# Where the embedding product of a transformer layer is computed: in the gate stage, or for nine of ten token tiles between the rounds of the attention

## The chip, the cores and the metric

The kernel runs on one core of one Trainium2 chip. Its time is the device time of one execution in microseconds (us). Three runs of the kernel before took 1705.35 to 1705.85 us, with a median of 1705.7 us. The engines are named as in the profile: PE is TensorE (matmuls; PEld are its weight loads), DVE is VectorE, ACT is ScalarE, POOL is GpSimd, and SP is SyncE, whose queue issues nearly all DMAs.

## The reference

One layer of a bidirectional encoder is applied to 1024 and 256 tokens of width 1024, all in float32. What matters here, cut short:

```python
h = h + concat(diff_attention, gqa_attention) @ w_out   # both from one input projection
h = h + square(relu(norm(h) @ w_ff1)) @ w_ff2
gate = sigmoid(norm(h) @ w_ple_gate)
h = h + gate * (p @ w_ple_proj)        # p: tokens x 256, w_ple_proj: 256 x 1024
y = norm(h)
```

The last product, `p @ w_ple_proj`, is the embedding product. It depends on two inputs alone, so it can be computed at any time.

## The kernel before, in words

There are ten token tiles of 128 tokens (TORD, line 851, is their order). Each float32 matrix product is made of three matmuls on operands that are split into a high and a low part: high by high, high by low, low by high. ScalarE makes the high part by a rounding copy, and VectorE or GpSimd the low part by a subtraction.

The stages follow each other: the input projections, the attention, the MLP's two products (done by a scheme with seven products in place of eight, and kept in DRAM in between), and the gate stage.

**The attention** (lines 515 to 1060) runs in rounds. `plan_unit` (line 600) puts the steps of each unit of 256 queries into numbered rounds: scores `sc` on TensorE (line 642), their maximum or distance penalty on VectorE (lines 655 and 659), exponentials on ScalarE (lines 664 and 667), the scaling by the sum on GpSimd (675, 681), transposes `tr` on TensorE (696), their split by ScalarE (702) and VectorE (707), and the product with the values, `av` (720). Loads of keys and queries are issued three rounds ahead of the scores that use them (line 633).

**The side work.** A round leaves TensorE time, since the other engines work on the scores. A generator, `side_work` (line 954), gives other matmuls for it: first the rest of the query and key projections, `qk_rest` (line 814, tile `psa`), then the output projection in two parts (line 887, tile `pso`), of which the second needs the finished attention. The main loop (line 1037) first emits the round's scores, transposes and softmax steps, then takes side work until the debt is paid, and then emits the `av` products and the ends. The debt is the round's cost on TensorE, plus a constant for each `av` step, times `RATIO` (0.43) for rounds under 160, and times `RATIO2` (0.6) after that. A `yield 0.0` of the generator ends the side work of the round. Whatever is left of the second part of the output projection runs after the attention (line 1213), together with the transposes of the MLP's input.

In what order each engine takes its instructions is decided when the program is built: a scheduler places each instruction by a simulated time and the program's order, and each engine then takes its own list in that order and waits at the head of it.

**The gate stage** (lines 1546 to 1633) takes one token tile after another. `gate_input` (line 1499) transposes the next tile's residual and splits it. `gate` (1568) makes 24 matmuls of 512 columns for each half of the tile (tile `psg`) and then a sigmoid on ScalarE, VectorE and GpSimd. `embed` (1588) makes the half's embedding product in PSUM, of six matmuls (tile `psp`). Its operands are the token tile of p, loaded and split in the loop (lines 1552 to 1557), and the two row blocks of the weight, which `proj_w` (1486) has split while the MLP ended. `add` (1598) multiplies the product by the gate (VectorE, line 1601), updates the residual and takes its squares. Then the tile is normalised and stored. The last tile is cut into three pieces, and its embedding products are placed behind its gate products.

## Time and profile before

| what | value |
|---|---|
| median of three runs | 1705.7 us |
| span of the profiled execution | 1703.2 us |
| TensorE busy | 1666.5 us (98%), 9849 matmuls |
| VectorE, ScalarE, GpSimd busy | 1177.2, 868.3, 658.4 us |
| score matmuls | from 196.3 us to 686.1 us |
| matmuls of the output projection | from 446.6 us to 753.9 us |
| gate matmuls | from 1547.1 us to 1690.5 us |
| moved by DMA | 278.28 MB |

The profile is that of one execution; its times count from the start of the span. The profiled execution has no time of its own beside the span; what lies around the span is read from the difference between the span and the runs' median, 2.5 us. A row of the groups gives busy time and the mean duration of one instruction, and behind a bar the idle time of the engine before it. The end of a matmul is modelled, and successive matmuls overlap, so that the time that one costs is read from how many fit into a stretch.

### The profile page before, as it was taken

Reading aid. Unit: us, or ns where it says so; the run is one execution under the profiler, and the core shown is the slowest. Engines: PE = TensorE matmul, PEld = TensorE weight load, DVE = VectorE, ACT = ScalarE, POOL = GpSimd, SP = SyncE. Lnnn points to the kernel's source line nnn. Section 1 sums busy time; section 2 is a strip of 40 time slices with the busy share of each in tenths; the row PEclk is TensorE's granted clock in tenths of the full one; section 3 lists DMA queues with packets and bytes.
Section 4 is the critical chain, followed back from the end, with each engine's and each line's share of the span. In section 5 each row is a group of like instructions: output and inputs, shape, how many; then the busy total and the mean of one; then the engine's idle time right before and its main releaser. Section 6 shows DMA issues by size and latency. Waiting matters only on the chain.

```text
span 1703.2 us, 27269 instructions
## 1 busy us (share of the span) xinstructions
PE 1666.5 (98%) x9849; PEld 1488.6 (87%) x9849; DVE 1177.2 (69%) x2119; ACT 868.3 (51%) x1749; POOL 658.4 (39%) x647
## 2 busy tenths in 40 slices
PE   8999999999899999999999999999999999999997
PEld 8999889888788888889999999998888888888886
DVE  7788588787887878578666666665655865445666
ACT  8543377677766767674333233333433333354644
POOL 1224455555653445424655666520533400001441
PEclk9999999999999999999999999999999999999999
DMA  9767844433953624495343434359666466532111
GB/s 316 228 225 246 233 141 124 138 92 108 269 156 118 165 69 127 134 308 181 132 156 127 138 131 150 122 198 376 202 216 195 130 205 193 169 114 73 35 44 50
DMA packets 191867, 278.28 MB, mean 163 GB/s; under 512 B 13674, under 2 KB 121076, under 8 KB 191732
## 3 DMA queue, kind: packets, MB, share of 16 engines
q1 hardware_dynamic: 189988, 271.28, 49.7%
q0 software_dynamic: 1600, 5.24, 1.0%
q8 instruction: 78, 1.28, 0.3%
q14 instruction: 57, 0.47, 0.1%
q10 hardware_dynamic: 144, 0.00, 0.0%
HBM read 182.63 MB, written 88.61 MB: 159 GB/s over the span
## 4 chain that ended last, share of the span: by engine, by line
PE 79%; DVE 7%; ACT 4%; issue 4%; DMA 3%; POOL 3%; SPq 0%; POOLq 0%; ACTq 0%; DVEq 0%
PE psa L255 6%; PE sc L642 5%; PE psb L255 5%; PE av L720 5%; PE pso L255 4%; PE tr L696 3%; PE psv L255 3%; PE psg L1576 2%; DVE pl L707 1%; DMA h_sb<-in_x 1%; DVE mm L659 1%; PE f__16295 L156 1%; PE f__15255 L156 1%; PE f__16637 L156 1%; PE f__15600 L156 1%
## 5 line engine op out<-in xcount | busy, mean ns | idle before, releaser
L1373 ACT ACTIVATE ao<-ar 128x1280 fp32r<-128x1280 f32 x56 | 71.3, 1275 | 187.5 <-PE f__16299 L156 37.8
L642 PE MATMUL sc<-kt,qt 128*128 128x512 f32 (+1 forms) x576 | 157.0, 392 | 6.9 <-ACT p L667 4.6
L707 DVE TENSOR_TENSOR pl<-tr,ph 128x512 fp32r<-128x512 f32 x204 | 137.9, 684 | 33.5 <-ACT ph L702 32.3
L1375 DVE TENSOR_TENSOR ao<-ar,ao 128x1280 fp32r<-128x1280 f32 x56 | 93.3, 1666 | 94.0 <-ACT ao L1373 94.0
L702 ACT ACTIVATE ph<-tr 128x512 fp32r<-128x512 f32 x204 | 119.8, 595 | 56.9 <-PE tr L696 50.4
L255 PE MATMUL pso<-ow,mt 128*128 128x512 f32 x480 | 119.4, 395 | 4.2 <-ACT ow L883 1.8
L696 PE MATMUL tr<-ident,p 128*128 128x128 f32 x768 | 116.0, 274 | 5.7 <-DVE pl L707 4.9
L642 PEld LDWEIGHTS sc<-kt,qt 128*128 128x128 f32 x576 | 99.4, 190 | 24.8 <-ACT p L667 6.1
L1576 PE MATMUL psg<-gw,n 128*128 128x512 f32 (+1 forms) x504 | 115.4, 384 | 0.0
L696 PEld LDWEIGHTS tr<-ident,p 128*128 128x128 f32 x768 | 91.8, 141 | 22.5 <-DVE pl L707 8.6
L1576 PEld LDWEIGHTS psg<-gw,n 128*128 128x128 f32 x504 | 90.8, 188 | 19.5
L255 PEld LDWEIGHTS pso<-ow,mt 128*128 128x128 f32 x480 | 87.5, 188 | 22.4 <-DVE osq L747 2.0
L1094 POOL TENSOR_SCALAR w1r<-w1r,gmlp 128x256 f32<-128x256 f32 x112 | 79.7, 728 | 67.6 <-DMA w1r<-in_w_ff 67.6
L720 PE MATMUL av<-ph,vt 128*128 128x256 f32 x544 | 102.4, 289 | 1.1 <-ACT ph L702 0.5
L681 POOL TENSOR_SCALAR p<-p,rl 128x1024 f32<-128x1024 f32 x64 | 76.0, 1188 | 51.3 <-DVE rl L679 46.6
L1167 ACT ACTIVATE w<-w1s 128x512 fp32r<-128x512 f32 x56 | 35.2, 628 | 116.5 <-POOL w1s L1174 49.4
L659 DVE TENSOR_REDUCE mm<-sc 128x1 f32<-128x1024 f32 (+1 forms) x80 | 84.2, 1055 | 8.8 <-PE sc L642 8.3
L720 PE MATMUL av<-pl,vt 128*128 128x256 f32 x408 | 89.5, 301 | 0.0
L720 PEld LDWEIGHTS av<-ph,vt 128*128 128x128 f32 x544 | 82.4, 190 | 6.6 <-ACT ph L702 0.9
L667 ACT ACTIVATE p<-sc,mm 128x1024 f32<-128x1024 f32 x64 | 71.3, 1114 | 25.5 <-DVE mm L659 18.5
L655 DVE CUSTOM_DVE_ANT_0 p<-sc,dist 128x1024 f32<-128x1024 f32 x64 | 77.6, 1218 | 7.9 <-PE sc L642 3.8
L664 ACT ACTIVATE p<-p,mm 128x1024 f32<-128x1024 f32 x64 | 73.5, 1149 | 18.0 <-DVE mm L655 17.3
(1520 smaller groups left out, 4717.2 us busy)
## 6 DMA issues: line engine op xcount, KB each, us to landing
ar<-ad SPq DMA_DIRECT2D x56, 640.0 KB, 4.0
w2r<-in_w_ff SPq DMA_DIRECT2D x56, 512.0 KB, 4.6
qt<-qd SPq DMA_DIRECT2D x160, 128.0 KB, 3.1
ad<-q SPq DMA_DIRECT2D x64, 320.0 KB, 3.0
ad<-qs SPq DMA_DIRECT2D x48, 320.0 KB, 2.2
w1r<-in_w_ff SPq DMA_DIRECT2D x28, 512.0 KB, 4.3
md<-ml SPq DMA_DIRECT2D x40, 256.0 KB, 2.5
mt<-md SPq DMA_DIRECT2D x20, 512.0 KB, 5.4
```

Of the source, the lines that this page charges most:

```text
L255: PE.matmul(ps, a, b, start=i == 0, stop=i == n - 1)
L642: PE.matmul(ps[:, h0:h0 + n], shared["q"][:, cc, v, i * P:(i + 1) * P], kt[:, s0 + h0:s0 + h0 + n], start=v == 0, stop=v == 1)
L655: V.tensor_tensor_reduce(out=p[:, :sn], in0=ps[:, :sn], in1=dst_t[:, off:off + sn], scale=SLOPES[idx], scalar=3.0e38, op0=ALU.add, op1=ALU ...
L659: V.tensor_reduce(out=st["m", i][:, 0:1], in_=ps[:, :sn], axis=AX.X, op=ALU.max, negate=True)
L681: G.tensor_scalar(p[:, :sn], p[:, :sn], rl[:, 0:1], 1.0, op0=ALU.mult, op1=ALU.mult)
L696: PE.transpose(t[:, jj, i * P:(i + 1) * P], st["ws"][i][:, j * P:(j + 1) * P], ident)
L702: S.activation(ph, st["tr", j2], AF.Copy)
L707: V.tensor_tensor(pl, st["tr", j2], f(st["ph", j2][:]), op=ALU.subtract)
L720: PE.matmul(st["av"][:, :256], x_, y_, start=j2 == 0 and n == 0, stop=j2 == nj - 1 and n == len(pr) - 1)
L1094: G.tensor_scalar(raw[:, k], raw[:, k], gmlp[:, 4 * kh + k:4 * kh + k + 1], 1.0, op0=ALU.mult, op1=ALU.mult)
L1375: V.tensor_tensor(ao[:, 1], a, f(ao[:, 0]), op=ALU.subtract)
L1576: ends[:] = [PE.matmul(ps, a, b, start=m == 0, stop=m == len(pr) - 1)]
```

## The change

A new generator, `embed_early`, stands in the side work between `qk_rest` and the output projection. It loads the projection weight by halves of 512 columns and pT by pairs of token tiles, splits them on ScalarE and GpSimd, makes the six matmuls of each tile and half (tile `pse`), evacuates the product from PSUM on ScalarE (tile `eo`), and stores it to `ed` in DRAM. It skips the token tile that the gate stage takes last. The gate stage loads each other tile's product into one of two slots (`et`) and multiplies by it from SBUF; it makes the embedding product itself for the last tile alone. The split of the weight for that tile moves from the end of the MLP into the gate stage. `RATIO` goes from 0.43 to 0.5. The early load of one part of the MLP's weight, which the main loop issued when the first output tile was done, is issued behind the attention if it has not been by then.

```diff
-    RATIO = 0.43
+    RATIO = 0.5
...
+    ed = dp.tile([NT, P, D], F32, name="ed")
+
+    def embed_early():
+
+        out = [wp.tile([P, 4, P], F32R, tag=tag, name="eo") for tag in ("wh", "wl")]
+        wt = [wp.tile([P, 4, P], F32R, tag=tag, name="ew") for tag in ("wh", "wl") * 2]
+
+        def half(n0):
+            for k in range(2):
+                raw = rawp.tile([P, 4, P], F32, tag="raw", name="rawe", bufs=2)
+                dma(raw, w_proj[k * P:(k + 1) * P, n0:n0 + 512].rearrange("p (a c) -> p a c", c=P))
+                yield 0.0
+                S.activation(wt[2 * k], raw, AF.Copy)
+                G.tensor_tensor(wt[2 * k + 1], raw, f(wt[2 * k][:]), op=ALU.subtract)
+
+        def tokens(t0):
+            raw = rawp.tile([P, 4, P], F32, tag="raw", name="rawe", bufs=2)[:].rearrange("p (k c) t -> p k (c t)", k=2)
+            dma(raw, pT[:, t0:t0 + 256].rearrange("(k p) t -> p k t", p=P))
+            hl = zp.tile([P, 2, 512], F32R, tag="zl", name="pe").rearrange("p v (k t) -> p v k t", k=2)
+            S.activation(hl[:, 0], raw, AF.Copy)
+            G.tensor_tensor(hl[:, 1], raw, f(hl[:, 0]), op=ALU.subtract)
+            return hl
+
+        w = [t[:].rearrange("p a c -> p (a c)") for t in wt]
+        pairs = [(n0, t0) for n0 in range(0, D, 512) for t0 in range(0, T, 256)]
+        hls = []
+        for i, (n0, t0) in enumerate(pairs):
+            if t0 == 0:
+                yield from half(n0)
+            while len(hls) < 2 and i + len(hls) < len(pairs):
+                hls.append(tokens(pairs[i + len(hls)][1]))
+            hl = hls.pop(0)
+            for u in range(2):
+                t = t0 // P + u
+                if t == LASTT:
+                    continue
+                c = slice(u * P, u * P + P)
+                ps = pj("pse")
+                pr = []
+                for k in range(2):
+                    pr += [(hl[:, 0, k, c], w[2 * k]), (hl[:, 0, k, c], w[2 * k + 1]), (hl[:, 1, k, c], w[2 * k])]
+                yield from mm_gen(ps, pr, 3)
+
+                def evac(ps=ps, t=t, n0=n0, o=out[u]):
+                    o = f(o[:].rearrange("p a c -> p (a c)"))
+                    S.activation(o, ps, AF.Copy)
+                    dma(ed[t, :, n0:n0 + 512], o)
+
+                if u == 0:
+                    evac()
+                else:
+                    deferred.append(evac)
+                    yield 0.0
...
     def side_work():
         yield from qk_rest()
+        yield from embed_early()
         flush()
...
     flush()
+    if not WN[0]:
+        w1_fetch(0, 1)
...
-            proj_w(0, AOS[m % 3])
-            proj_w(1, WOS[m % 3])
             n3[FORD[1]] = gate_input(FORD[1])
...
-        pr_ = gq_.tile([P, 2, P], F32, tag="pr", name="pr")
-        dma(pr_, pT[:, t * P:(t + 1) * P].rearrange("(k p) t -> p k t", p=P))
-        p_h = gq_.tile([P, 2, P], F32R, tag="p_h", name="p_h")
-        p_l = gq_.tile([P, 2, P], F32R, tag="p_l", name="p_l")
-        S.activation(p_h, pr_, AF.Copy)
-        G.tensor_tensor(p_l, pr_, f(p_h[:]), op=ALU.subtract)
+        if last:
...
+        else:
+            et = slot(("W11", "W10")[ti % 2], [P, D], F32, "et")
+            dma(et, ed[t])
+            if ti in (3, 4):
+                proj_w(ti - 3, (AOS, WOS)[ti - 3][(NM - 2) % 3])
...
-                add(i, gate(i), embed(i))
+                add(i, gate(i), et[:, i * 512:i * 512 + 512])
```

Three places of the order show the move. The first is TensorE where the query and key projections have ended. In the kernel before, some rounds of the attention (`sc`, `tr`, `av`) follow alone, and then the output projection, `pso`, comes in small pieces:

```order
L642 MATMUL sc<-kt,qt 128x512 x4
L696 MATMUL tr<-ident,p 128x128 x4
L720 MATMUL av<-pl,vt_3166 128x256 x2
L255 MATMUL pso<-ow,mt 128x512 x4
L720 MATMUL av<-ph,vt_3166 128x256 x2
L696 MATMUL tr<-ident,p 128x128 x4
L720 MATMUL av<-pl,vt_3166 128x256 x2
L642 MATMUL sc<-kt,qt 128x512 x4
L255 MATMUL pso<-ow,mt 128x512 x3
```

In the changed kernel the embedding products, `pse`, six matmuls of one tile and half at a time, stand between rounds there, and the output projection begins after the last of them:

```order
L642 MATMUL sc<-kt,qt 128x512 x4
L696 MATMUL tr<-ident,p 128x128 x4
L255 MATMUL pse<-ew,pe 128x512 x6
L696 MATMUL tr<-ident,p 128x128 x4
L720 MATMUL av<-ph,vt_3167 128x256 x2
L720 MATMUL av<-pl,vt_3167 128x256 x2
L720 MATMUL av<-ph,vt_3167 128x256 x2
L720 MATMUL av<-pl,vt_3167 128x256 x2
L720 MATMUL av<-ph,vt_3167 128x256 x2
L255 MATMUL pse<-ew,pe 128x512 x6
L642 MATMUL sc<-kt,qt 128x512 x4
```

All 108 `pse` matmuls stand among the attention's; of the 480 matmuls of `pso`, 192 stood behind the last score matmul before, and 240 do now.

The second place is TensorE in the gate stage. Here is one token tile before, with the transposes of the next tile (`trg`), two times 24 gate matmuls (`psg`), and behind each half the six of the embedding product (`psp`):

```order
L1506 MATMUL trg<-ident,hq 128x128 x8
L1576 MATMUL psg<-gw,n_17548 128x512 x24
L156 MATMUL psp<-pw,p_h 128x512 x2
L156 MATMUL psp<-pw,p_l 128x512
L156 MATMUL psp<-pw,p_h 128x512 x2
L156 MATMUL psp<-pw,p_l 128x512
L1576 MATMUL psg<-gw,n_17548 128x512 x24
```

Three tiles of the changed kernel, in the same stage:

```order
L1638 MATMUL psg<-gw,n_17123 128x512 x48
L1564 MATMUL trg<-ident,hq 128x128 x8
L1638 MATMUL psg<-gw,n_17184 128x512 x48
L1564 MATMUL trg<-ident,hq 128x128 x8
L1638 MATMUL psg<-gw,n_17341 128x512 x48
```

The twelve embedding matmuls of a tile are gone, and the two halves follow each other at once.

The third place is the queue of SyncE in the gate stage, where the loads of the embedding product (`et`) stand between the stores of the result (`y`):

```order
L1617 DMA et<-ed 128x1024
L1695 DMA y<-hq 128x512 x2
L1617 DMA et<-ed 128x1024
L1695 DMA y<-hq 128x512 x2
L1617 DMA et<-ed 128x1024
```

Before, the smaller loads of pT stood there. The first two `et` loads are issued earlier, the first of them during the MLP; the others keep this alternation, so that each waits in the queue behind a tile's stores.

More of the change, by code (lines that the diff above doesn't have):

```diff
@@ L851, in encoder_kernel @@
     TORD = (0, 1, 2, 3, 8, 9, 4, 5, 6, 7)
+    LASTT = TORD[NT - 2]
     def h_row(t):
@@ L1551, in encoder_kernel @@
         n3h, n3l, rn = n3.pop(t)
-        pr_ = gq_.tile([P, 2, P], F32, tag="pr", name="pr")
-        dma(pr_, pT[:, t * P:(t + 1) * P].rearrange("(k p) t -> p k t", p=P))
-        p_h = gq_.tile([P, 2, P], F32R, tag="p_h", name="p_h")
-        p_l = gq_.tile([P, 2, P], F32R, tag="p_l", name="p_l")
-        S.activation(p_h, pr_, AF.Copy)
-        G.tensor_tensor(p_l, pr_, f(p_h[:]), op=ALU.subtract)
+        if last:
+            pr_ = gq_.tile([P, 2, P], F32, tag="pr", name="pr", bufs=1)
+            dma(pr_, pT[:, t * P:(t + 1) * P].rearrange("(k p) t -> p k t", p=P))
+            p_h = gq_.tile([P, 2, P], F32R, tag="p_h", name="p_h", bufs=1)
+            p_l = gq_.tile([P, 2, P], F32R, tag="p_l", name="p_l", bufs=1)
+            S.activation(p_h, pr_, AF.Copy)
+            G.tensor_tensor(p_l, pr_, f(p_h[:]), op=ALU.subtract)
+        else:
[3 more added lines that the diff above has]
+                proj_w(ti - 3, (AOS, WOS)[ti - 3][(NM - 2) % 3])
         pieces = [(0, 512), (512, 512)] if not last else [(0, 512), (512, 256), (768, 256)]
         ss = gq_.tile([P, 3], F32, tag="fss", name="fss")
-        banks = [[bank("f2", "psg"), pj("psg")], [bank("f1", "psp"), bank("f1", "psp")]]
+        banks = [[bank("f2", "psg"), pj("psg")]]
         if last:
             banks[0].append(pj("psg"))
-            banks[1].append(bank("tr", "psp"))
+            banks.append([bank("f1", "psp"), bank("f1", "psp"), bank("tr", "psp")])
         ends = []
```

## The prediction

> **What bounds the kernel now.** I read the page first, then busy time by stage, then the waits of TensorE, then the gate stage by itself. The page's span, busy row and slices:
>
> ```profile
> span 1703.2 us, 27269 instructions
> PE 1666.5 (98%) x9849; PEld 1488.6 (87%) x9849; DVE 1177.2 (69%) x2119; ACT 868.3 (51%) x1749; POOL 658.4 (39%) x647
> PE   8999999999899999999999999999999999999997
> ```
>
> The median of the runs, 1705.7 us, is 2.5 us over this span; I forecast the span and add 2.5. TensorE is never long idle, so moving its work elsewhere gains nothing unless it lands in time that TensorE now waits. Busy time by stage (stretch, length, then busy us of each engine, granted clock, DMA share) shows where such time is:
>
> ```profile
> core 0: us, PE busy (x) PEld busy (x) DVE busy (x) ACT busy (x) POOL busy (x), PEclk, DMA share, GB/s
> 196.00:433.00 237.00, 231.38 (x1461) 203.62 (x1459) 186.67 (x346) 166.78 (x340) 126.42 (x132) 1.00 0.46 134
> 433.00:465.00 32.00, 27.28 (x162) 22.92 (x161) 25.53 (x43) 23.62 (x48) 22.90 (x22) 0.95 1.07 287
> 465.00:690.00 225.00, 217.10 (x1328) 188.19 (x1327) 184.00 (x352) 157.00 (x327) 101.68 (x112) 1.00 0.43 126
> 690.00:713.00 23.00, 22.03 (x142) 19.02 (x142) 11.58 (x23) 12.63 (x31) 10.38 (x15) 1.00 0.42 138
> 713.00:755.00 42.00, 42.00 (x211) 35.47 (x210) 25.26 (x58) 29.64 (x66) 17.09 (x23) 1.00 0.94 300
> 1546.00:1686.00 140.00, 140.00 (x643) 114.45 (x642) 88.13 (x155) 70.28 (x187) 48.79 (x40) 1.00 0.11 40
> ```
>
> The four first rows are the attention with its side work, 517 us, of which TensorE is busy 497.8: 19.2 us idle. The rest of the output projection (713 to 755) and the gate stage (1546 to 1686) have none. A matmul's modelled end overlaps the next one's start: 434 matmuls of 512 columns fill 100 us, 0.230 us each, where one row lasts 0.395.
>
> ```profile
> 1200.00:1300.00 100.00, 100.00 (x434) 81.19 (x433) 60.63 (x37) 37.67 (x39) 40.01 (x18) 1.00 0.65 206
> L156 PE MATMUL psp<-pw,p_h 128*128 128x512 f32 x76 | 24.0, 395 | 0.0
> L156 PE MATMUL psp<-pw,p_l 128*128 128x512 f32 x38 | 15.0, 394 | 0.0
> ```
>
> So each wait hides 0.165 us more than the idle time shows; some 40 waits of the attention cost about 19.2 + 40 x 0.165 = 26 us (the 40 are my count, an estimate). That is the most that filling can win. Three views say when they occur: the longest waits of TensorE in 196 to 713 (us in total, times, longest); four stretches of 12 us in busy time by stage; the same four for TensorE's side matmuls alone (line 255):
>
> ```profile
> PE tr L696 <- DVE pl L707: 5.1, 9, 1.1
> PE sc L642 <- ACT p L667: 4.6, 6, 1.7
> PE sc L642 <- DVE mm L655: 2.1, 7, 0.5
> ```
> ```profile
> 360.00:372.00 12.00, 10.29 (x71) 8.89 (x71) 9.62 (x17) 8.24 (x16) 3.00 (x4) 1.00 0.35 111
> 396.00:408.00 12.00, 10.96 (x70) 9.33 (x68) 10.95 (x26) 11.03 (x27) 7.18 (x8) 1.00 0.43 133
> 576.00:588.00 12.00, 12.00 (x74) 10.56 (x73) 9.79 (x18) 7.63 (x15) 3.40 (x4) 1.00 0.37 100
> 624.00:636.00 12.00, 12.00 (x75) 10.64 (x75) 10.85 (x22) 7.52 (x18) 4.79 (x7) 1.00 0.32 97
> ```
> ```profile
> 360.00:372.00 12.00, 0.00 (x0) 0.00 (x0) 1.00 0.35 111
> 396.00:408.00 12.00, 0.00 (x0) 0.00 (x0) 1.00 0.43 133
> 576.00:588.00 12.00, 4.28 (x18) 3.34 (x19) 1.00 0.37 100
> 624.00:636.00 12.00, 5.38 (x23) 4.00 (x23) 1.00 0.32 97
> ```
>
> With 18 or 23 side matmuls in 12 us TensorE does not wait; with none it waits 1.7 and 1.0 us, for VectorE and ScalarE, which then set the pace of a round. The waits sit where the side stream is dry.
>
> **The gate stage: 24.8 us off TensorE.** The 76 + 38 products of 512 columns less the last tile's 6 are 108; 108 x 0.230 = 24.8 us. TensorE had no idle time here, so it goes in full if the other engines keep up. One tile is a stretch of 14.7 us:
>
> ```profile
> 1614.70:1629.40 14.70, 14.70 (x70) 11.99 (x69) 9.60 (x17) 7.06 (x20) 6.46 (x6) 1.00 0.13 45
> 1688.20:1703.00 14.80, 5.54 (x42) 5.06 (x40) 9.49 (x25) 6.63 (x19) 0.00 (x0) 0.81 0.19 71
> ```
>
> Without 12 x 0.230 = 2.8 us a tile takes 11.9; VectorE's 9.60 becomes the next late thing, but fits. The new load of 512 KB has a tile's time: the first two are issued ahead of the stage, each later one behind the y stores of two tiles earlier, some 13 us before its use (an estimate: one and a half tiles of 11.9 less the 5 us of chain between multiply and store), and the 640 KB loads of the MLP land in 4.0 us. What a late load would hold up is the multiply on VectorE, and behind it the next tile's residual.
>
> ```profile
> ar<-ad SPq DMA_DIRECT2D x56, 640.0 KB, 4.0
> ```
>
> At the end, the last tile's chain of VectorE and ScalarE starts 2.8 us earlier but queues behind that of the tile before (VectorE 9.49 of the last 14.8 us): I give back 1.0, bounds 0 and 2.8. The projection weight's two splits move a few tiles later on engines with room: nothing.
>
> **Output projection: +11.0 us.** In the order, 192 of its matmuls stand behind the last score matmul before, 240 now: 48 x 0.230 = 11.0 us more in the stretch from 713 on, where TensorE is 42.00 of 42.00 busy. The moved load of w1 has those 50 us to land: nothing.
>
> **Attention: +13.8 us of work, less what falls into waits.** The 108 products come in (24.8) and 48 matmuls go out (11.0). I took the order of TensorE's instructions, gave each its interval, 0.230 us for 512 columns, 0.12 for 256 ((0.64 - 0.40)/2 in the rows below) and 0.11 for 128 (8 in 1.03, of which the last's overlap is some 0.16),
>
> ```profile
> 701.21 1.03 PE L696 MATMUL tr<-ident,p 128*128 128x128 f32 x8
> 702.79 0.64 PE L720 MATMUL av<-ph,vt 128*128 128x256 f32 x4
> 703.27 0.40 PE L720 MATMUL av<-pl,vt 128*128 128x256 f32 x2
> ```
>
> and took every run of attention matmuls with no side matmul in it: the parts beyond 6 us add up to 92 us before and 61 now. Ratio 0.5 makes the projections denser, though two dry runs stand where one stood (13 us ahead of the products, 9 behind them, for 10). If waits go with dry time, 26 x 61/92 = 17 stay: a gain of 9. Bounds: 0 (waits depend on the engines' bursts, not on side work) and 26.
>
> The products load ScalarE: 14 splits and 18 evacuations, at 632 and 688 ns, 21.2 us; GpSimd takes 14 x 1.290 = 18.1.
>
> ```profile
> L883 ACT ACTIVATE ow<-h_sb x12: 616/632/635, 441.7 to 641.9; 128x512 fp32r<-128x512 f32 x12
> L884 POOL TENSOR_TENSOR ow<-h_sb,ow x12: 1259/1290/1302, 446.8 to 643.8; 128x512 fp32r<-128x512 f32 x12
> ```
> ```profile
> L1580 ACT ACTIVATE ge<-psg,grn 128x512 f32<-128x512 f32 x18 | 12.4, 689 | 34.1 <-PE psg L1576 34.1
> ```
> ```profile
> 465.00:690.00 225.00, 69.29 (x277) 50.46 (x278) 15.80 (x23) 1.00 0.43 126
> ```
>
> From 465 to 690 TensorE has 277 side matmuls (64 us), so 153 us of attention of its own, to ScalarE's 157: 1.02 to 1. The products lie among 54 us of attention: ScalarE 54 x 1.02 + 21.2 = 76, TensorE 54 + 24.8 = 79. ScalarE never did better than 11.03 of 12 us (the stretch at 396); at that 92% it needs 83, so 4 us over. I take 3; bounds 0 (the bursts even out) and 13 (83%, 92 us). Behind an evacuation on ScalarE are queued the attention's exponentials and splits, and for them TensorE waits.
>
> The SyncE queue gets 32 more issues (4 weight pieces, 10 token tiles, 18 stores). A store waits for its evacuation, behind it are query and key loads, which are issued three rounds ahead: 204 rounds in 517 us make 7.6 us, and the DMA share is 0.43. Nothing; if that cover went, a score matmul would wait the 3.1 us in which such a load lands, once per late store.
>
> ```profile
> L707 DVE TENSOR_TENSOR pl<-tr,ph 128x512 fp32r<-128x512 f32 x204 | 137.9, 684 | 33.5 <-ACT ph L702 32.3
> ...
> qt<-qd SPq DMA_DIRECT2D x160, 128.0 KB, 3.1
> ```
>
> **The sum.** -24.8 + 11.0 + 13.8 - 9 + 3 + 1 = -5 us: 1698.2 of span, 1700.7 us. The work of TensorE is the same before and after; the forecast is nothing but filled waits less two small prices.
>
> **The rivals.** (a) *No wait is filled*, because the new side work comes with ScalarE work of its own and an extra dry run. Then -24.8 + 24.8 + 3 + 1 = +4 at most, 0 without the prices: 1705.7 to 1709.7, mostly no change. For it: the waits are short, 9 for 5.1 us; against it: the pairs of 12 us above. (b) *Most waits are filled.* -26 x 0.7 + 4 = -14: 1691.7. For it: 24.8 us nearly match 26; against: runs of over 4.5 us without side work are 24 in the new order as in the old, only shorter. (c) *ScalarE becomes the bound among the products* and runs at no more than the 74% that it shows from 433 to 465 (23.62 of 32): 76/0.74 = 103 us for 79, +24; less 9, plus 1: slower, 1722. It decides from 87% downward, where its 8 us eat the gain. At the 83% it is +13 - 9 + 1: 1710.7. (d) *The multiply in the gate stage is blocked.* It read PSUM and one tile in SBUF; now both operands are in SBUF. An instruction of one element per partition on line 143, with only SBUF operands, shows what can happen:
>
> ```profile
> L143 DVE SCALAR_TENSOR_TENSOR rfv<-rf,rfv x10: 211/1076/1317, 1570.9 to 1698.0; 128x1 f32<-128x1 f32 x10
> ```
> ```profile
> 1647.27 1.31 DVE L143 SCALAR_TENSOR_TENSOR rfv<-rf,rfv 128x1 f32<-128x1 f32 x1 [0.93 <-ACT rf L140]
> 1647.28 1.29 POOL L1584 TENSOR_TENSOR gd<-gd,ge 128x512 f32<-128x512 f32 x1 [2.07 <-ACT rf L140]
> ```
>
> It takes 0.21 us alone, 1.31 while GpSimd runs. If both multiplies of a tile lose 1.29 us so, VectorE needs 9.60 + 2.6 = 12.2 us a tile for TensorE's 11.9, and with its own waits a tile would take some 13: 9 x 1.1 = 10 us back, 1710.7. Against it: GpSimd works 6.46 of 14.7 us, and its next step mostly waits for this multiply. The Trainium skill, SBUF — State Buffer, Who interferes with whom, states that a VectorE instruction with two SBUF inputs contends with a GpSimd instruction that reads SBUF, and that the later one is blocked until the first ends; it speaks against this change. By that rule, these rows agree.
>
> **Chances.** Forecast with its bounds 0.52, (a) 0.25, (b) 0.08, (c) 0.08, (d) 0.07. Within 0.2% (3.4 us, about what a measurement of this kernel can tell from no change) lie part of (a) and the forecast's upper edge. Faster: 0.44 + 0.08 = 0.52; same: 0.08 + 0.18 + 0.02 = 0.28; slower: 0.07 + 0.08 + 0.05 = 0.20. The range reaches from (b) to (a)'s end, 1691 to 1710; the forecast alone spans 1694 to 1706.
>
> **What would show it.** Right: the gate stage 24 us shorter with TensorE still without gaps; the stretch behind the attention 11 us longer; the attention with its products longer by 5 to 10 us, not 14, and idle under 14 us of 19. Wrong: idle time of TensorE in the attention unchanged or larger, released by ScalarE among the products; multiplies of over 0.69 us on VectorE and gaps of TensorE in the gate stage.

## The result and the profile after

The changed kernel took 1715.36 us (median of 4 runs, 1711.9 to 1716.09), the kernel before 1705.53 us beside it (4 runs, 1702.18 to 1705.85). The ratio is 1.0058, 95% interval 1.0044 to 1.0072: slower by some 10 us, where 1700.7 us, 5 us faster, was forecast. The profiled execution of the changed kernel took 1711.9 us, at the low end of its runs, so that the profiles hold 6.9 of the 9.8 us between the two medians; the rest stands in no trace. The page's span, its busy row and TensorE's slices:

```profile
span 1710.1 us, 27376 instructions
PE 1669.7 (98%) x9849; PEld 1492.5 (87%) x9849; DVE 1171.8 (69%) x2119; ACT 882.2 (52%) x1772; POOL 672.4 (39%) x652
PE   8999999999999999999999999999999999999997
```

The span is 6.9 us longer. Between the same landmarks in both traces (first and last score matmul, last matmul of the output projection, first and last gate matmul, end) the difference divides so: +1.7 ahead of the first score matmul, +15.0 in the attention, +14.3 from there to the end of the output projection, +0.3 in the MLP, -25.2 in the gate stage, +0.8 in the tail. (The 1.7 arise before 67 us, where both kernels issue the same instructions; I count it as scatter between executions: over all runs whose work ahead of the attention is the same, the first score matmul starts between 195.6 and 200.1 us.) Busy time by stage of the changed kernel, the products' stretch (420 to 510) and the two changes of side work around it apart:

```profile
198.00:420.00 222.00, 216.41 (x1347) 190.45 (x1345) 170.08 (x317) 153.16 (x313) 121.04 (x125) 0.99 0.47 138
420.00:510.00 90.00, 86.74 (x528) 74.70 (x529) 66.23 (x117) 72.19 (x145) 50.70 (x52) 1.00 0.61 178
510.00:545.00 35.00, 30.50 (x179) 25.73 (x179) 26.04 (x54) 26.95 (x60) 25.46 (x25) 0.95 0.98 281
545.00:707.00 162.00, 157.15 (x954) 136.98 (x953) 132.24 (x240) 105.19 (x216) 73.94 (x81) 1.00 0.42 120
707.00:731.00 24.00, 22.57 (x141) 19.21 (x140) 12.62 (x25) 13.32 (x32) 11.20 (x15) 1.00 0.20 67
731.00:786.00 55.00, 53.11 (x257) 44.31 (x256) 28.59 (x74) 34.44 (x77) 16.08 (x22) 0.97 0.89 283
786.00:806.00 20.00, 18.02 (x110) 17.52 (x109) 18.61 (x28) 16.74 (x30) 0.75 (x1) 0.91 0.55 194
1578.00:1692.00 114.00, 114.00 (x531) 93.49 (x530) 78.66 (x151) 67.66 (x178) 42.15 (x32) 1.00 0.22 74
```

The first five rows are the attention, 533 us, with TensorE busy 513.4: 19.6 us idle, where before it was 19.2 of 517. So none of the idle time was filled. The sixth row is new: TensorE, which had 42.00 busy of 42.00 behind the attention, now has a gap there. The gate stage, last row, is without gaps and 25 us shorter, as forecast. TensorE's longest waits from 196 to 731 us (total, times, longest):

```profile
PE tr L696 <- DVE pl L707: 4.8, 9, 1.4
PE sc L642 <- ACT p L667: 3.4, 2, 2.4
PE pso L255 <- DVE osq L747: 2.3, 2, 1.3
PE pso L255 <- DVE o L768: 1.6, 1, 1.6
PE av L720 <- DVE o L768: 1.4, 1, 1.4
```

The waits for the splits `pl` are as many and as long as before (9 for 5.1). Those for the exponentials `p` became fewer, and waits for the ends of a unit (`osq`, `o`) grew instead. The new gap behind the attention, in order of time:

```profile
756.15 0.81 SPq L1046 DMA_DIRECT2D hd<-h_sb  x1
...
762.72 1.15 ACT L1070 ACTIVATE h_sb<-h_sb,nst 128x1024 f32<-128x1024 f32 x1 [5.77 <-DMA hd<-h_sb]
...
763.92 1.50 PE L1164 MATMUL trn<-ident,h_sb 128*128 128x128 f32 x8 [1.89 <-ACT h_sb L1070]
```

A tile's residual is stored (`hd`), and ScalarE may scale it in place only when that store has read it; ScalarE waits 5.77 us at the head of its list, and TensorE's next transposes 1.89 us for ScalarE. The DMA issues of that stretch, 731 to 786 us (number, size, median us to landing), and then those of the kernel before from 713 to 755:

```profile
w<-wed SPq DMA_DIRECT2D x8, 512.0 KB, 6.3
hd<-h_sb SPq DMA_DIRECT2D x8, 512.0 KB, 6.7
mt<-md SPq DMA_DIRECT2D x6, 512.0 KB, 6.1
```
```profile
hd<-h_sb SPq DMA_DIRECT2D x6, 512.0 KB, 7.5
w<-wed SPq DMA_DIRECT2D x6, 512.0 KB, 5.8
mt<-md SPq DMA_DIRECT2D x4, 512.0 KB, 6.7
```

With 240 output matmuls behind the last score matmul for 192, eight of these stores, eight weight loads and six loads of `mt` fall into the stretch for six, six and four. Per us that is as many as before, 8 in 55 us for 6 in 42, so the stretch is longer and not denser.

One more measure is used below. **Lost time** is, from the first score matmul to the first matmul behind the last transpose `trn`, the sum over all TensorE matmuls of the time to the next one's start, less what its columns take (0.230 us for 512, 0.173 for 384, 0.117 for 256, 0.109 for 128). It holds waits, what a wait hides of overlap, and lower clock alike, for one profiled execution each, and its values are good to some 0.7 us. Before it is 43.9 us, after 49.5.

The lower clock is found in short stretches alone. From the first score matmul to 20 us behind the last transpose, the changed kernel's trace has four, each 3.41 us long at half clock (the column before the last two), and that of the kernel before has one:

```profile
358.30:361.70 3.40, 3.40 (x16) 3.21 (x15) 1.90 (x4) 0.71 (x2) 2.52 (x3) 0.50 0.30 91
518.70:522.10 3.40, 3.40 (x15) 3.11 (x14) 1.26 (x3) 2.25 (x4) 3.40 (x5) 0.50 1.11 344
764.40:767.80 3.40, 3.40 (x13) 2.81 (x12) 3.37 (x9) 2.06 (x5) 2.02 (x3) 0.51 0.52 153
795.20:798.60 3.40, 3.40 (x16) 3.30 (x14) 3.40 (x4) 2.98 (x7) 0.00 (x0) 0.50 0.00 0
```
```profile
461.80:465.20 3.40, 3.40 (x12) 2.81 (x11) 3.40 (x6) 1.20 (x3) 0.74 (x1) 0.50 1.04 326
```

By the measure above 6.3 us are lost in the four and 1.7 in the one. So 4.6 of the 5.6 us that the changed kernel loses more in these two executions come from the clock, behind waits of TensorE of 1.1 to 2.0 us; outside such stretches it loses 43.2 us for 42.2.

### The profile page after: what moved, and what is told of

The parts are those of the page before. It is cut to its first block, busy times and chain, and to the rows that moved or that the text cites. A ratio compares the mean times of both kernels' runs of the same rounds, so it can differ in the third digit from the quotient of the medians.

```text
span 1710.1 us, 27376 instructions
## 1 busy us (share of the span) xinstructions
PE 1669.7 (98%) x9849; PEld 1492.5 (87%) x9849; DVE 1171.8 (69%) x2119; ACT 882.2 (52%) x1772; POOL 672.4 (39%) x652
## 3 DMA queue, kind: packets, MB, share of 16 engines
q1 hardware_dynamic: 194724, 283.21, 51.6%
## 4 chain that ended last, share of the span: by engine, by line
PE 78%; DVE 7%; ACT 5%; DMA 5%; issue 3%; POOL 2%; SPq 0%; POOLq 0%; ACTq 0%; DVEq 0%
PE psa L255 6%; PE sc L642 5%; PE av L720 5%; PE tr L696 4%; PE psb L255 3%; PE pso L255 3%; PE psv L255 2%; PE psg L1638 2%; PE pse L255 1%; DMA hd<-h_sb 1%; DMA xt<-in_x 1%; ACT ph L702 1%; DVE p L655 1%; PE f__16530 L156 1%; PE f__15490 L156 1%
## 5 line engine op out<-in xcount | busy, mean ns | idle before, releaser
L681 POOL TENSOR_SCALAR p<-p,rl 128x1024 f32<-128x1024 f32 x64 | 78.3, 1224 | 49.4 <-DVE rl L679 45.2
```

The source lines that it names most:

```text
L681: G.tensor_scalar(p[:, :sn], p[:, :sn], rl[:, 0:1], 1.0, op0=ALU.mult, op1=ALU.mult)
```

## The experiments

Eighteen runs, all against the kernel before on the same chip. The suspects after the result: the ratio by itself (the first expectations call it B), ScalarE's load, the crowd behind the attention (E), and the products' place. "In the changes" is the part of the lost time that falls into the stretches between one kind of side work and the next: projections to products, products to output projection, first half of it to second. "Dry" is the prediction's measure, attention work beyond 6 us without side work, in us.

| run | kernel | median us | ratio [95%] | lost | in the changes | dry |
|---|---|---|---|---|---|---|
| | before (0.43) | 1704.2 to 1705.5 | 1 | 43.9 | 7.1 | 92 |
| e17 | before, 0.40 | 1708.07 | 1.0017 [1.0008, 1.0026] | 47.1 | 7.9 | 93 |
| e16 | before, 0.46 | 1719.36 | 1.0086 [1.0072, 1.0099] | 54.8 | 8.2 | 95 |
| e1 | before, 0.50 | 1714.99 | 1.0052 [1.0039, 1.0064] | 52.8 | 18.6 | 88 |
| e7 | before, 0.50 then 0.43 | 1724.15 | 1.0106 [1.0087, 1.0124] | 65.0 | 21.2 | 87 |
| e8 | no products, 0.43 | 1679.95 | 0.9843 [0.9827, 0.9859] | 42.5 | 6.8 | 92 |
| e2 | no products, 0.50 | 1688.64 | 0.9906 [0.9892, 0.9921] | 50.5 | 17.0 | 88 |
| | after (0.50) | 1715.36 | 1.0058 [1.0044, 1.0072] | 49.5 | 12.3 | 61 |
| e5 | after, 0.43 | 1727.7 | 1.0122 [1.0104, 1.0140] | 65.0 | 22.6 | 85 |
| e10 | after, 0.47 | 1713.93 | 1.0053 [1.0040, 1.0065] | 52.2 | 13.8 | 80 |
| e9 | after, 0.49 | 1711.0 | 1.0030 [1.0020, 1.0041] | 51.6 | 7.7 | 75 |
| e4 | after, 0.60 | 1715.36 | 1.0063 [1.0049, 1.0076] | 51.9 | 10.9 | 57 |
| e3 | after, evacuation on VectorE | 1710.75 | 1.0037 [1.0024, 1.0051] | 47.9 | 11.6 | 57 |
| e6 | e5, evacuation on VectorE | 1727.09 | 1.0128 [1.0107, 1.0149] | 65.1 | 25.6 | 87 |
| e12 | after, no pauses | 1710.12 | 1.0027 [1.0017, 1.0038] | 49.4 | 13.4 | 54 |
| e11 | e5, `mt` loaded ahead | 1723.01 | 1.0104 [1.0090, 1.0118] | 61.1 | 16.7 | 85 |
| e15 | 0.49, no pauses, VectorE | 1711.86 | 1.0040 [1.0028, 1.0053] | 51.6 | 11.0 | 77 |
| e18 | 0.45, all four | 1717.14 | 1.0078 [1.0065, 1.0092] | 56.1 | 8.2 | 78 |
| e13 | products as a block first, 0.43 | 1729.55 | 1.0146 [1.0132, 1.0160] | 63.6 | 8.1 | 86 |
| e14 | e13, less work ahead | 1724.53 | 1.0114 [1.0099, 1.0130] | 58.0 | 4.7 | 84 |

### The two halves of the change apart (e1, e2)

e1 is the kernel before with the new ratio alone.

```diff
-    RATIO = 0.43
+    RATIO = 0.5
```

> The kernel before with RATIO 0.5 and nothing else; 168 matmuls of the output projection then stand behind the last score matmul, 192 before. Theory A (the waits of TensorE in the attention keep their share of some 3 to 4% whatever side work runs): no change, within 3 us of before. Rival B (the denser side work of the changed kernel is what cost it): slower by 4 us or more. My theory on record (waits go with time without side work: 88 us beyond 6 us here, 92 before): 1 us faster, not to be told from A.

1714.99 us: the ratio alone costs what the whole change costs. Busy time of e1 in its two changes of side work, then TensorE's side matmuls alone in the same stretches, then the kernel before in its own two:

```profile
402.00:431.00 29.00, 22.84 (x139) 18.03 (x137) 22.25 (x45) 22.60 (x48) 23.71 (x22) 1.00 0.94 255
615.00:651.00 36.00, 30.41 (x194) 25.28 (x193) 30.89 (x54) 28.39 (x59) 24.95 (x26) 1.00 0.42 121
```
```profile
402.00:431.00 29.00, 0.78 (x7) 0.57 (x5) 1.00 0.94 255
615.00:651.00 36.00, 0.87 (x4) 0.43 (x3) 1.00 0.42 121
```
```profile
433.00:447.00 14.00, 11.47 (x75) 9.58 (x74) 13.16 (x22) 12.77 (x27) 10.43 (x12) 1.00 1.03 294
640.00:657.00 17.00, 15.24 (x98) 12.90 (x96) 14.94 (x35) 14.46 (x33) 10.28 (x11) 1.00 0.56 154
```

With 0.50 the projections and the first half of the output projection are used up earlier, while the heads that the next part needs come no earlier. The changes become 29 and 36 us long for 14 and 17, and 11.8 us of TensorE's time are idle in them for 4.3. The clock is no part of it: in its one stretch at half clock e1 loses 1.9 us, the kernel before 1.7.

e2 is the changed kernel without the products of nine tiles; the gate stage reads rows of x in their place.

```diff
-        yield from embed_early()
...
-            dma(et, ed[t])
+            dma(et, x[t * P:(t + 1) * P, :])
```

> The changed kernel without the generator of the embedding product; the gate stage loads rows of x in its place, so that the product is left out for nine tiles. It has the attention of e1 and the gate stage of the changed kernel. Theory A: the gate stage alone is worth 24 to 25 us against e1, so 1680 to 1682 us, and the embedding products and what they displace cost 33 to 35 us in the changed kernel, 8 to 10 more than the 24.8 that they take on TensorE. Rival C (the gate stage gives part of its gain back through blocked multiplies or late loads): 20 us or less against e1.

1688.64 us, over the 1680 to 1682 of theory A, since the ratio had cost what that theory left out. Against e1 the gate stage gives 26.4 us; against the changed kernel the products cost 26.7, for 24.8 us of matmuls. At this ratio the products on balance fill nothing and lose little.

### Smaller terms (e3, e4)

e3 evacuates the products on VectorE. e4 raises the ratio to 0.60, so that 192 output matmuls stand behind the last score matmul as before the change.

```diff
-                    S.activation(o, ps, AF.Copy)
+                    V.tensor_scalar(o, ps, 1.0, None, op0=ALU.mult)
```
```diff
-    RATIO = 0.5
+    RATIO = 0.6
```

> The changed kernel with the 18 evacuations of the embedding products on VectorE in place of ScalarE, 12 us less ScalarE work in the attention. Rival D (ScalarE among the products is what costs): faster than the changed kernel by 4 us or more, and the stretch of the products shorter by as much. Theory A: within 3 us of the changed kernel, since TensorE is idle 3.3 of 90 us there, no more than elsewhere.

> The changed kernel with RATIO 0.6: 192 matmuls of the output projection behind the last score matmul as in the kernel before, 240 in the changed kernel. Theory E (part of the loss, some 3 us, is the wait of 1.9 us and the slower clock in the output projection behind the attention, where norm steps and their stores are crowded): that wait is gone and the kernel is 2 to 4 us faster than the changed one. Theory A alone: within 2 us of the changed one. The theory on record (dry time 57 us, 61 in the changed one): 1 us faster.

e3: 1710.75 us, some 4 less, about the 3 us that the prediction charged ScalarE; but the two intervals overlap (1.0024 to 1.0051 and 1.0044 to 1.0072), so the gain isn't clear of noise. e4: 1715.36 us. The crowd behind the attention is smaller there (8.0 us lost from the second half's first matmul on, for 11.0), and the products' stretch loses 11.2 us for 5.4. What was saved in one place was lost in another, which came back in e9 and e18. Nor does the crowd's size set its price: lost from the same matmul on are 2 us in e10, with 252 output matmuls behind the last score matmul, 8.3 in the kernel before with 192, and 10.5 in e1 with 168 (my counts). Suspect E is not borne out.

### The changed kernel at the old ratio (e5, e6, e11)

```diff
-    RATIO = 0.5
+    RATIO = 0.43
```

> The changed kernel with the side stream's ratio back at 0.43; the embedding products stay in the attention. In the order 300 output-projection matmuls now stand behind the last score matmul, and dry runs beyond 6 us add up to 85 us (61 with 0.5). Theory R (the loss is the ratio's: with 0.5 the side stream runs dry in more places, and the 108 products only move): about the kernel before, 1703 to 1708 us. Theory P (the products' place costs the loss: a second change from one kind of side work to the next, and the norm steps crowded behind the attention): 1712 us or more, and more than the changed kernel, since the stretch behind the attention grows again by 60 x 0.230 = 14 us while the attention shrinks by less. Theory D (waits go with dry time, as the prediction had it): 61 to 85 us of dry time brings 26 x 24/92 = 7 us: 1722 us.

> As the run with ratio 0.43, and the 18 evacuations of the embedding products on VectorE instead of ScalarE. With ratio 0.5 this move was worth 4 to 5 us. Theory R: 1699 to 1704 us, so a little faster than the kernel before. Theory P: 1708 us or more. If what the evacuations cost at 0.5 was itself a matter of the pace, no gain over the run with ratio 0.43 alone.

1727.7 and 1727.09 us. My theory R, that the loss was the ratio's, fell: the ratio that suits the kernel before is the worst that the changed one had. Two of TensorE's waits of e5 from 196 to 740 us are among the longest of all runs:

```profile
PE pso L255 <- DMA mt<-md: 7.7, 1, 7.7
...
PE av L739 <- DMA mt<-md: 3.2, 1, 3.2
```

The second half of the output projection starts behind the attention there; its first tile of attention output is loaded only then, and no attention work covers the load. The other is at 571 us, where the first half starts. The profile names a DMA that came last, but that matmul reads what ScalarE makes; ScalarE's rows in order of time there:

```profile
568.65 1.36 ACT L938 ACTIVATE ow<-wor 128x512 fp32r<-128x512 f32 x2 [2.83 <-DMA wor<-in_w_out]
569.92 0.58 ACT L702 ACTIVATE ph<-tr 128x512 fp32r<-128x512 f32 x1
570.40 0.37 ACT L734 ACTIVATE osq<-av 128x256 f32<-128x256 f32 x1
```

A weight split of the start waits 2.83 us at the head of ScalarE's list for its load, and the attention's steps (`ph`, `osq`) stand behind it. Moving the evacuations (e6) changed nothing at this ratio.

e11 loads that first tile two token tiles earlier, into a slot that is free because the tiles' slots are rotated by one (those lines are left out here):

```diff
...
+            elif it == 8:
+                if all((ch, 0) in md_done for ch in (2, 3, 6, 7)):
+                    mts2[0] = slot("W7", [P, 4, 2, P], F32R, "mt")
+                    dma(f(mts2[0][:]), md[1][:, :, :, TORD[0] * P:(TORD[0] + 1) * P])
```

> The run with ratio 0.43 (1727.7 us), with the first tile of attention output for the second half of the output projection loaded two token tiles ahead (its slots rotated by one, so that the one it needs is free). Theory T: the wait of 7.7 us between the halves goes, 1719 to 1721 us. Rival: the load only waits for the last head, or the next thing (weight splits, the second tile's load) is late instead: 1724 to 1728 us.

1723.01 us, between the two expectations: the 7.9 us lost at this change are gone, and 2.6 more are lost behind it and 1.9 more ahead of the first half.

### Where the loss sits (e7, e9, e10, e12)

By then I held that the loss sits in the changes (theory T). e7 takes the kernel before with 0.50 up to round 90:

```diff
-        owed += max((cost + lead) * (0.0 if r <= 6 else RATIO if r < LATE else RATIO2), LEAD.get(r, 0.0))
+        owed += max((cost + lead) * (0.0 if r <= 6 else (0.5 if r < 90 else RATIO) if r < LATE else RATIO2), LEAD.get(r, 0.0))
```

> The kernel before with ratio 0.5 up to round 90 and 0.43 from there to round 160. The change from the query and key projections to the output projection is as dry as with 0.5 throughout (19 us of attention work in a row; 9.7 in the kernel before), but the second dry stretch, around 625 us, should go. Theory R, with the two stretches each worth what their extra waits showed (4.3 us and 6.2 us of the 9.9): 1709 to 1711 us. If the second stretch alone counts: 1705 us. If neither and the ratio acts in another way (less cover at the end of the attention): 1714 us.

1724.15 us, worse than both ratios that it is made of. The second change stayed long (30 us, 11.4 lost), and behind it 17.7 us are lost for 8.3 before.

e9 and e10 are the changed kernel with 0.49 and 0.47, e12 has no pauses in the start of the output projection:

```diff
-    Y = (0, 1, 1)
+    Y = (0, 0, 0)
```

> The changed kernel with ratio 0.49. Theory T (what is lost is lost where the side stream changes from one kind of work to the next: TensorE's lost time in those stretches was 7.1 us in the kernel before, 12.3 in the changed one, 22.6 with ratio 0.43, against 36.8, 37.2 and 42.4 in all the rest): the attention work that passes without side work in the three changes is 3.2 + 9.8 + 8.7 us, where the changed kernel has 13.1 + 9.2 + 8.4; at the losses measured per us (0.33, 0.7 and 0.3) 2.6 us faster than the changed kernel, 1712 to 1713 us. Theory R (the ratio itself, on the line from 0.50 at 1715 to 0.43 at 1728): 1717 us. Theory D (all dry time beyond 6 us, 75 us for 61): 1719 us.

> The changed kernel with ratio 0.47, which moves the changes of side work the other way: 13.6 + 15.8 + 7.4 us of attention work without side work in them. Theory T: 4.5 + 11.1 + 2.2 us lost there, 4.6 more than in the changed kernel, 1719 to 1721 us, and 7 us slower than with 0.49. Theory R: 1721 us, 4 us slower than with 0.49. Theory D (80 us of dry time for 61): 1720 us, 1 us slower than with 0.49.

> The changed kernel without the pauses of a round each that the start of the output projection makes between its weight splits and before its first matmul (Y all 0). Dry attention work in the three changes 13.1 + 6.0 + 4.1 us for 13.1 + 9.2 + 8.4. Theory T in the form that it is the missing side work that costs: 3 to 4 us faster, 1711 to 1712 us. In the form that the start's own loads and splits cost (ScalarE, in order, waits for a weight load with the attention's exponentials behind it): no gain or some us slower, 1715 to 1720 us.

1711.0, 1713.93 and 1710.12 us. e9 came out as theory T said, but not for its reason: the changes lose 4.6 us less than in the changed kernel and all the rest 6.7 more. (The profiled executions of the two took the same, 1712.02 and 1711.9 us, so the traces can't tell where the 4 us between the medians lie; of the 2 us between those of e12 and the changed kernel, all lie ahead of the first score matmul.) e10 lost 1.5 us more in the changes than the changed kernel, where 4.6 were expected, and missed its 1719 to 1721. In e12 the start of the output projection has 6 us of attention work for 9.2 and loses as much as in the changed kernel (6.1 us for 6.0), most of it in one wait; TensorE's longest of 505 to 520 us:

```profile
PE pso L255 <- DMA mt<-md: 4.2, 1, 4.2
```

### Is the loss the schedule's alone? (e8, e13 to e18)

e8 is e2 with ratio 0.43, so the attention of the kernel before with the gate stage of the changed one.

> Leaves out the embedding product of nine token tiles (their rows of the input are loaded in its place), ratio 0.43: the attention of the kernel before with the gate stage of the changed one. Theory R: 1705 less 25 to 26 us, 1679 to 1681 us, and 8 to 10 us faster than the same with ratio 0.5. The difference to the run with ratio 0.43 and the products is what the products cost among the rounds: 25 us if nothing is filled and nothing lost, under 20 if they fill waits, over 30 if their place costs.

1679.95 us, as theory R had it. Its busy time in the attention's second part and behind the attention stands beside the rows of before (217.10 of 225, 42.00 of 42):

```profile
465.00:690.00 225.00, 216.60 (x1325) 187.53 (x1324) 184.36 (x352) 157.19 (x327) 101.91 (x112) 1.00 0.43 127
...
713.00:755.00 42.00, 42.00 (x212) 35.52 (x211) 25.52 (x58) 29.73 (x66) 16.95 (x23) 1.00 0.94 300
```

With the schedule unchanged the lost time is unchanged too, 42.5 us for 43.9. The gate stage alone is worth the 25 us. But the products at this ratio cost 47.8 us (e5 less e8): 24.8 of work and 22.5 of new lost time.

e13 keeps that schedule, with the ratio 0.43, and puts the products ahead of the rounds, as one block; e14 leaves half of the projection work that stood there for the rounds (`PRE` 7000 for 14000).

```diff
-        yield from embed_early()
...
+    for _ in embed_early():
+        flush()
     owed = PRE
```

> The changed kernel with its embedding products issued as one block ahead of the attention's first rounds instead of between the query and key projections and the output projection, and ratio 0.43. In the order the side work of all later rounds stands as in the kernel before (9.7 and 13.3 us of dry attention work at the two changes, 192 output-projection matmuls behind the last score matmul). Theory S (the loss is the schedule that the products force on the side work; the products by themselves only move 24.8 us): the attention's lost time is that of the kernel before, 43 to 46 us, and the time 1704 to 1708 us, within 0.2% of before. Rival (the way through DRAM, the loads and the splits cost by themselves, wherever the products stand): 1711 us or more. If the block covers waits of the first rounds: under 1702 us.

> As the block ahead of the rounds, but half of the projection work that the kernel puts ahead of the first round (some 7 us, 30 matmuls) is left for the rounds, since the products stand there now. In the order the changes of side work become shorter (9.5 and 6.6 us of dry work for 9.7 and 13.3), 228 output-projection matmuls stand behind the last score matmul. Theory S with the losses per us of dry work as measured: 2 us faster than the block alone. If the first rounds need that cover: 3 to 7 us slower than the block alone. From the runs so far, in which what one stretch saved came back in another (0.49: 4.6 us less in the changes, 6.6 more elsewhere), I take no difference as likely as either.

1729.55 and 1724.53 us: the rival's number. e14 is 5 us faster than e13, more than any of its expectations had. From the output projection's first matmul on, e13 loses 26.7 us to 26.8 before: same order, same loss, which is the part of theory S that held. Ahead of that it loses over 20 us more: some 17 around the block (3.9 of them ahead of the first score matmul, so not in the table) and some 6 in the projections behind it, whose order the block moves against the heads. Busy time in the block's last part, and TensorE's longest waits from 180 to 240 us:

```profile
210.00:240.00 30.00, 23.50 (x93) 15.20 (x92) 12.07 (x22) 16.88 (x32) 16.32 (x14) 1.00 0.88 246
```
```profile
PE pse L255 <- ACT eo L857: 3.0, 4, 1.7
PE sc L642 <- DMA rawe<-in_pT: 2.0, 1, 2.0
PE pse L255 <- ACT pe L831: 1.9, 2, 1.4
```

A block has nothing to cover its own loads, splits and evacuations, and ScalarE takes them in one list with the first rounds' exponentials. Diluted among the rounds (the changed kernel) the products' stretch loses 5.4 us in 85.

e15 joins the three small gains, e16 and e17 move the ratio of the kernel before to 0.46 and 0.40, and e18 is the order with the shortest changes that I found (0.45, no pauses, `mt` ahead, evacuation on VectorE).

> The changed kernel with ratio 0.49, without the pauses, and with the evacuations of the products on VectorE. Each by itself was 4 to 5 us faster than the changed kernel (1711.0, 1710.1, 1710.8 for 1715.4). If they add up: 1702 us, faster than the kernel before. If each only moved the schedule from a high to a usual place: 1708 to 1712 us.

> The kernel before with ratio 0.46 for 0.43, nothing else. If the kernel before sits at a low point of its ratio (0.43 gave 1705, 0.5 gave 1715, 0.5 up to round 90 and then 0.43 gave 1724): 1709 us or more. If the time rises smoothly with the ratio from 1705 at 0.43 to 1715 at 0.50: 1709 us as well, so only a value over 1712 or under 1707 speaks for jumps.

> The kernel before with ratio 0.40, nothing else: 24 more output-projection matmuls behind the last score matmul (216 for 192), dry attention work at the two changes 9.7 + 14.7 us for 9.7 + 13.3. Theory S (0.43 is a low point of the schedule, paces around it lose more): 1709 to 1720 us. Rival (a lower ratio is simply better, and the change lost because it raised it): 1700 to 1706 us.

> The changed kernel with ratio 0.45, no pauses, the first tile of the second half loaded ahead, and the products' evacuations on VectorE: of all orders looked at the one with the least dry attention work at the changes, 5.1 + 4.5 + 0 us (13.1 + 9.2 + 8.4 in the changed kernel). Theory T (the loss sits in the changes): 12.3 us lost there become 4 or less, 1703 to 1707 us. Theory S (what the changes save comes back elsewhere, as with 0.49): 1709 to 1720 us.

1711.86, 1719.36, 1708.07 and 1717.14 us. The gains of e3, e9 and e12 don't add up. The kernel before stands at a low point of its ratio: 1708, 1705, 1719 and 1715 us at 0.40, 0.43, 0.46 and 0.50. (Toward 0.40 it is shallow, 0.17%, and e17 lies between its two expectations.) At 0.46 its changes lose 8.2 us, hardly more than its 7.1; the loss is in waits among the rounds, as in TensorE's longest of e16:

```profile
PE sc L642 <- ACT p L667: 9.9, 6, 4.0
```

e18 lost 8.2 us in the changes for 12.3 in the changed kernel, and 47.9 elsewhere for 37.2. Theory T fell with it. Of the versions that make the products, none is as fast as the kernel before; the best is e12, slower by 0.27%.

**What the runs show together.** Moving the products moves 24.8 us of TensorE work from a stage without gaps into the attention, and neither pair of runs that differs by the products alone (e2 and the changed kernel, e8 and e5) shows waits taking any of it up on balance. Beside that the lost time goes where the schedule takes it: 43.9 to 65.0 us in five paces of the kernel before, 47.9 to 65.1 in eleven versions with the products among the rounds. The kernel before is at the low end of its own scale; the change leaves that point. How the 10 us divide between the ratio and the products depends on which is taken first. With the ratio first (e1, e2) it costs some 9 us, the gate stage gives 26.4 and the products cost 26.7. With the products first (e8, e5) they cost 47.8, and the ratio then gives some 11 back. Nor is it the same loss: e1 loses in waits at the changes (18.6 us for 7.1), the changed kernel's trace mostly at half clock (6.3 us for 1.7).

Why a given order loses 44 us or 65 is not settled: neither dry work nor the length of the changes tells it, and I found no count in the order that does. The clock is a part of it, from nothing in e8 and 1.6 us in e16 to 12.7 in e11. Nor was it tried whether a search over all of the scheduler's constants finds the changed kernel a point as low; with a lost time of 44 us it would by estimate be level with the kernel before, not faster.

## Why the prediction was wrong, point by point

- **Gate stage, -24.8.** Right: -25.2, no gaps. The multiplies took no longer than before (691 ns there too). Their group in the changed kernel, duration as least, median and most in ns:

```profile
L1663 DVE TENSOR_TENSOR ge<-et,ge x18: 679/691/693, 1592.1 to 1692.2; 128x512 f32<-128x512 f32 x18
```

  And the landing of the loads of the product, least, median and most, in the view of that tile; TensorE and VectorE never waited for one:

```profile
DMA to landing us min/median/max: 3.1/3.2/4.7
```

  Rival (d) did not come, because its condition did not: no multiply ran at the same time as a GpSimd instruction. So no run shows here what the Trainium skill (SBUF — State Buffer, Who interferes with whom) states of two such SBUF readers, beyond line 143, which again took 0.21 to 1.31 us.
- **Tail, +1.** Right: +0.8.
- **Output projection behind the attention, +11.0.** The moved work is right; 3.3 us came on top, about TensorE's wait of 1.89 us there and the stretch at half clock right behind it, in which 1.6 us are lost. The step counted matmuls alone. That the crowd of norm steps and stores brings such a loss is not shown (e10 above).
- **Attention, +13.8 of work.** Right: the span grew by 15.0, 1.2 over the work, so the work came in full; the 1.2 is no more than the one stretch at half clock that the attention has more (two for one, 1.4 us).
- **"If waits go with dry time, 26 x 61/92 = 17 stay: a gain of 9."** This is the step that failed. Dry time fell to 61 us and the idle time went from 19.2 to 19.6, so the gain was nothing, as the prediction's own sign of being wrong had it. (Among the products TensorE was idle for 3.3 of 90 us, mostly until ScalarE was done; that is no larger share than in the whole attention.) Over the table it tells nothing: 92 us with 43.9 lost, 95 with 54.8, 87 with 65.0, 61 with 49.5, 54 with 49.4. The two pairs of 12 us windows that carried it compared places that differ in more than side work. That the side work was dry there because the stage was at a hard point, and not the other way round, is my reading; no run tests it.
- **The bounds of that step, 0 and 26.** The loss side was cut off at nothing, with the reason that waits "depend on the engines' bursts, not on side work". They depend on both: the ratio alone, which I counted as a help, cost 0.52%, some 9 us (e1). A price of the lower clock behind short waits was no term of the sum at all; it is 4.6 us in the trace. A price for a changed schedule, taken from nothing but its scatter, needed to reach to about 20 us.
- **ScalarE, +3.** The size is near what e3 gave at 0.50 (some 4), but e6 and e15 gave nothing, so it is not settled as a cost of its own. An evacuation took 598 ns for the 688 assumed, as its group in the changed kernel shows:

```profile
L857 ACT ACTIVATE eo<-pse x18: 578/598/601, 424.0 to 507.2; 128x512 f32<-128x512 f32 x18
```

- **SyncE queue and later loads, nothing.** Right within the products' stretch: no score matmul waited for a late store. Not right for `mt`: where the order of the side work moved, its loads were waited for, up to 7.7 us (e5).
- **The sum.** In the span, forecast -5 and measured +6.9: 7.2 of the difference in the attention (the 9 not gained, while the rest came out 1.8 lower), 3.3 behind it, 1.7 ahead of it, the rest cancels. Rival (a), no wait filled, was nearest in its mechanism, and stopped at 1709.7, for want of a new loss; the 1710.7 us of (c) at 83% and of (d) stood nearer in number, by mechanisms that did not come. The sum went from span to time by 2.5 us; the changed kernel's median lies 5.3 us over the span of its profile.

## What to carry to other kernels

Work that moves between two stages of a saturated engine costs what it saves, so such a change lives from waits alone; ask what would fill them, and don't take a low share of side work at a wait for its cause. A paced schedule may stand at a low point, as this one did: whatever shifted its order paid the distance to another point, here 3 to 20 us with the same work, and that distance belongs on the loss side of the range. Turning one pacing constant of the kernel before by a step or two measures this scatter at once, before a few microseconds are forecast for a reordering.

## What the hardware showed that I had not expected

- A ratio changed by 0.03 moved the time up by some 15 us (0.43 to 0.46) or 3 us (to 0.40), with the same instructions in another order.
- A mean granted clock of 0.91 to 0.97 (510 to 545, 731 to 786 and 786 to 806 us) was one stretch of 3.41 us at half clock in an otherwise full one. I divided the traces of all twenty kernels from 200 to 820 us into windows of 3.41 us in step with these stretches. Of the windows at full clock, each of the 40 in which TensorE was busy for less than 43% was followed by one at half clock, none of the 3293 with 61% or more was, and 11 of the 54 between. (Busy time is by the modelled ends.) At half clock matmuls of 256 columns started 0.21 us apart (at 360 us of the changed kernel) for 0.12.
- A DMA of 512 KB took 3.2 us to land in the gate stage (DMA share 0.22) and 6.1 to 6.7 behind the attention (0.89).
- The evacuation of 128x512 from PSUM took 598 ns on ScalarE and 682 on VectorE (e3).
